# Hybrid encoder trunk: the two PSUM banks of an up chunk read as one tile, and one convolution tap on ScalarE

## The chip, the cores and the metric

The kernel runs on one core of one Trainium2 chip. The metric is device time in microseconds; lower is better. Before the change, three runs gave 2391.53, 2390.47 and 2388.43 us, median 2390.47.

## What is computed

Two layers over 256 tokens of width 2048, in float32. Each layer normalises, mixes the tokens (a bidirectional mLSTM in the first, a bidirectional gated linear recurrence, HGRN2, in the second), adds the result to the residual `h`, normalises again and goes through a gated MLP with a convolution. The change is in that MLP:

```python
def conv_glu(hn, w_up, conv_w, conv_b, w_down):
    u = hn @ w_up                                  # 2048 -> 2 x 5504
    a, v = jnp.split(u, 2, axis=-1)
    ap = jnp.pad(a, ((0, 0), (1, 1), (0, 0)))
    c = conv_b
    for j in range(3):
        c = c + ap[:, j:j + s] * conv_w[j]
    return (jax.nn.gelu(c, approximate=False) * v) @ w_down   # 5504 -> 2048
```

A final normalisation closes the trunk.

## The kernel before

**Arithmetic.** Every float32 operand of a product is split in a high and a low part in the fp32r format. ScalarE makes the high part by a cast (`parts`, L137), VectorE the low part by a subtraction (L138); products are high x high, high x low and low x high. The split activations lie in tiles of 512 columns, high parts first.

**Chunks.** The program is a list of chunks that `stream` (L282) walks through. A chunk is one output block over the whole inner dimension. In a "tm" chunk the tokens are rows of the output (L344). In a "fm" chunk the features are rows, 2 x 128 of them: for each of 16 blocks of the inner dimension and each half f, L328 multiplies the high part of the weights by both parts of the activations (512 columns: the main sum in the first 256, the low correction in the last 256), and L332 the low part of the weights by the high part (256 columns, added to the first 256). An "st" chunk is a down product by a seven-product scheme (L226 to L280), which uses all four banks of the pool `psm` and all four of `psa`.

**Weights.** Weight blocks of 2048 columns come by DMA through three `raw` buffers. They are split in pieces of 1024 columns into tiles `wh` and `wl`, four buffers of each, three pieces ahead of the matmuls (`LOOK`). A piece is four inner blocks of a fm chunk.

**PSUM.** `psm` has four tiles of one bank. A fm or tm chunk takes two of them, one per half, so that the next chunk fills the other two while the first two are read.

**Up chunks.** Each of the 86 up chunks (43 per layer, in halves of 22 and 21) gives 128 features of the gate `a` (half 0) and the same 128 of `v` (half 1). When its matmuls are recorded, `done_up`'s `go` (L1111) records the evacuation. Twice `fm_scaled` (L358): ScalarE copies the last 256 columns of the bank to SBUF (L355), VectorE adds the first 256 to it (L356) and multiplies by R, the reciprocal norm of each token (L361). Then VectorE makes the middle tap with the bias (L1118) and adds the left and right taps (L1119, L1120), ScalarE applies Gelu (L1121), VectorE multiplies by `v` (L1122), and the result is split for the down product (L1124, L1125). After some odd chunks `token_sums` (L527) makes the sums of tokens that the seven-product scheme needs.

**Beside it.** During the up chunks a side job (`prepare`, L573) loads down weights (`pth`), forms their sums on VectorE (L179 to L184) and stores them in `tscr`; the down chunks read them back. Their second splits are L209 and L210 (`th`, `tl`).

**Order.** Side jobs are stepped by `side.tick` while matmuls are recorded. What is recorded is not the order of execution: the framework's scheduler places the instructions of each engine by its own estimate of when they can run, with dependencies by tile; only instructions passed through `pin` and the loads through `late` keep the recorded order. Each engine then executes its list in order. The order of matmuls inside a fm chunk is partly set by hand with `swap` lists.

**Stages** of the profiled execution, roughly: first mixer to 380 us, up and down of layer 0 to 1092, second mixer to 1605 and its output product to 1680, up and down of layer 1 to the end. Up chunks fill 380 to 622, 746 to 986, 1680 to 1924 and 2034 to 2272.

Of the kernel before, what the change touches and what calls it, by code (L numbers as in the profile page):

```python
# [8 lines left out]
F32 = mybir.dt.float32  # L9
# [6 lines left out]
P = 128  # L16
T = 256
# [43 lines left out]
def trunk_kernel(ctx, tc, xT, x_d, fg_d, pp_d, cst_d, w_gate, w_first, w_aq, w_ak, w_av, w_ao, w_aout, w_ao2,  # L61
# [4 lines left out]
    keep = ctx.enter_context(tc.tile_pool(name="keep", bufs=1))  # L66
    wpool = ctx.enter_context(tc.tile_pool(name="wpool", bufs=1))
    ev = ctx.enter_context(tc.tile_pool(name="ev", bufs=1))
    psm = ctx.enter_context(tc.tile_pool(name="psm", bufs=4, space=PSUM))
    psa = ctx.enter_context(tc.tile_pool(name="psa", bufs=4, space=PSUM))  # L70

    pp = keep.tile([P, NPP], F32, name="pp")
# [113 lines left out]
    def split_squares(ch, parts):  # L186
# [26 lines left out]
        for u in range(units):  # L213
# [7 lines left out]
            if 2 * u + 1 < ch.nk:  # L221
                m = 512 if u in ch.seven else 1024
                wh, wl = parts(r[:, 1024:1024 + m], m)
                yield wh, wl, sums.pop(u, None)

    def squares_by_seven(ch, fetch, ready):  # L226

        psm_ = [psm.tile([P, 512], F32, tag="mm", name="mm") for _ in range(4)]
        P1, P6, P7, P5 = psm_
        C11, C12, C21, C22 = psa_ = [aux("pc") for _ in range(4)]  # L230
        begun = set()
        held.append(ch)

        def product(ps, x, w, stop):
            (xh, xl), (wh, wl) = x, w
            for i, (a, b) in enumerate(((xh, wh), (xh, wl), (xl, wh))):
                pe.matmul(ps, a, b, start=id(ps) not in begun, stop=stop and i == 2)  # L237
                begun.add(id(ps))

        def half(x, t):  # L240
            return x[:, t * P:(t + 1) * P], x[:, T + t * P:T + (t + 1) * P]

        def block(p, i):
            return tuple(w[:, i * 512:(i + 1) * 512] for w in p)

        units, last = (ch.nk + 1) // 2, max(ch.seven)
        for u in range(units):
            fetch()
            p = ready.pop(0)
            end = u == units - 1  # L250
            if 2 * u + 1 == ch.nk:
                x = ch.x(2 * u)
                for ps, t, w in ((C11, 0, 0), (C12, 0, 1), (C21, 1, 0), (C22, 1, 1)):
                    product(ps, half(x, t), block(p[:2], w), True)
                side.tick(2.7)
                break
            fetch()
            q = ready.pop(0)
            x0, x1 = ch.x(2 * u), ch.x(2 * u + 1)
            A11, A21, A12, A22 = half(x0, 0), half(x0, 1), half(x1, 0), half(x1, 1)  # L260
            B11, B22, B21 = block(p[:2], 0), block(p[:2], 1), block(q[:2], 0)
            if u in ch.seven:
                sx, t = ch.sums(u), q[2]
                S1, S3, S2, S4 = ((sx[:, i * P:(i + 1) * P], sx[:, 512 + i * P:512 + (i + 1) * P]) for i in range(4))
                T1, T3, T2, T4 = (block(t[i // 2], i % 2) for i in range(4))
                for i, (ps, x, w) in enumerate(((P1, A11, B11), (C12, S4, B22), (C11, A12, B21), (P5, S1, T1),
                                                (P7, S3, T3), (P6, S2, T2), (C21, A22, T4))):
                    product(ps, x, w, u == last and ps in psm_)
                    side.tick(0.65)
                if u == last:  # L270
                    ch.mid(psm_)
                continue
            B12 = block(q[:2], 1)
            for ps, (x, w), (y, v) in ((C11, (A11, B11), (A12, B21)), (C12, (A11, B12), (A12, B22)),
                                       (C21, (A21, B11), (A22, B21)), (C22, (A21, B12), (A22, B22))):
                product(ps, x, w, False)
                product(ps, y, v, end)
                side.tick(1.3)
        held.pop()
        ch.done(psa_)  # L280

    def stream(chunks):  # L282
        pieces = split_weights(chunks)
        ready = []

        def fetch():
            p = next(pieces, None)
            if p is not None:
                ready.append(p)

        for _ in range(LOOK):
            fetch()
        for ch in chunks:
            if ch.before:
                ch.before()
            if ch.kind == "st":
                squares_by_seven(ch, fetch, ready)
                continue
            ps = [psm.tile([P, 512], F32, tag="mm", name="mm") for _ in range(2)]
            k = 0  # L300
            while k < ch.nk:
                fetch()
                wh, wl, n = ready.pop(0)
                if ch.last and k + sum(p[2] for p in ready) + n == ch.nk:
                    pieces_, k0 = [(wh, wl, n)] + ready, k
                    for t in range(2):
                        k = k0
                        for wh, wl, n in pieces_:
                            for kk in range(n):
                                x, c = ch.x(k), slice(kk * 512, (kk + 1) * 512)  # L310
                                xh, xl = x[:, t * P:(t + 1) * P], x[:, T + t * P:T + (t + 1) * P]
                                pe.matmul(ps[t], xh, wh[:, c], start=False, stop=False)
                                pe.matmul(ps[t], xh, wl[:, c], start=False, stop=False)
                                pe.matmul(ps[t], xl, wh[:, c], start=False, stop=k == ch.nk - 1)
                                k += 1
                        ch.half(ps[t], t)
                    return
                if ch.kind == "fm":
                    ops = [(kk, f, part) for kk in range(n) for f in range(2) for part in "hl"]
                    for i in ch.swap:  # L320
                        i -= 2 * k
                        if 0 <= i < 2 * n - 1:
                            ops[2 * i + 1:2 * i + 3] = ops[2 * i + 2], ops[2 * i + 1]
                    for kk, f, part in ops:
                        x = ch.x(k + kk)
                        c = kk * ch.width + f * P
                        if part == "h":
                            pe.matmul(ps[f], wh[:, c:c + P], x, start=k + kk == 0, stop=False)  # L328
                            continue
                        if f:  # L330
                            side.tick(0.65)
                        pe.matmul(ps[f][:, 0:T], wl[:, c:c + P], x[:, 0:T], start=False, stop=k + kk == ch.nk - 1)  # L332
                    k += n
                    continue
                for kk in range(n):
                    x = ch.x(k)
                    st, sp = k == 0, k == ch.nk - 1
                    c = slice(kk * 512, (kk + 1) * 512)
                    ops = [(t, i) for t in range(2) for i in range(3)]
                    if ch.first and st:  # L340
                        ops.sort(key=lambda o: (0, 2, 1)[o[1]])
                    for t, i in ops:
                        a, w = ((0, wh), (0, wl), (T, wh))[i]
                        pe.matmul(ps[t], x[:, a + t * P:a + (t + 1) * P], w[:, c], start=st and i == 0, stop=sp and i == 2)  # L344
                    side.tick(1.3)
                    k += 1
            ch.done(ps)

    def split(dst, src, gcol, pin=lambda ins: ins):
        pin(act.activation(dst[:, 0:T], src, AF.Copy, scale=gcol))  # L350
# [746 lines left out]
    def ffn(layer, norm, nxt):  # L1097
# [12 lines left out]
        def done_up(f, i, GT, SX, seven):  # L1110
            def go(ps):  # L1111
                mp, R = box["mp"], norm.R
                avc = temporary(mp, "avc")
                a, v, c = (avc[:, j * T:(j + 1) * T] for j in range(3))
                fm_scaled(ps[0], R, a)
                fm_scaled(ps[1], R, v)
                cw = [col("conv_w", (layer * 3 + w) * FT + f) for w in range(3)]
                dve.tensor_scalar(c, a, cw[1], col("conv_b", layer * FT + f), ALU.mult, ALU.add)  # L1118
                dve.scalar_tensor_tensor(c[:, 1:T], a[:, 0:T - 1], cw[0], c[:, 1:T], ALU.mult, ALU.add)  # L1119
                dve.scalar_tensor_tensor(c[:, 0:T - 1], a[:, 1:T], cw[2], c[:, 0:T - 1], ALU.mult, ALU.add)  # L1120
                act.activation(c, c, AF.Gelu)  # L1121
                dve.tensor_tensor(c, c, v, ALU.mult)  # L1122
                g = slot(i, "g", mp)
                act.copy(g[:, 0:T], c)  # L1124
                dve.tensor_tensor(g[:, T:2 * T], c, g[:, 0:T].bitcast(F32), ALU.subtract)  # L1125
                GT.append(g)
                if i % 2 and i // 2 in seven:
                    SX[i // 2] = token_sums(mp, seven.index(i // 2), box["c"], c, avc[:, 0:2 * T])
                box["c"] = c
            return go  # L1130
# [157 lines left out]
```

## Time and profile before

| | |
|---|---|
| runs, us | 2391.53, 2390.47, 2388.43 |
| median, us | 2390.47 |
| span of the profiled execution, us | 2388.5 |
| time of that execution beyond its span | not given |
| instructions | 37988 |
| HBM read / written, MB | 512.69 / 39.91 |
| granted TensorE clock, mean | 0.999 |

The span runs from the first to the last instruction. Engines are PE (matmul), PEld (weight load, beside PE), DVE (VectorE), ACT (ScalarE), POOL (GpSimd) and SP (which issues DMAs). In a group's row stand the line, engine, operation, output<-input, sizes and count, then busy us, mean ns of one, and the idle time of the engine just before such instructions with what ended it. In a waits row stand who waited, for whom, total us, number and longest. A row of the windows view gives the stretch, its length, each engine's busy us with the number of its instructions, the granted clock, the DMA engines' share and GB/s. Matmuls overlap, and a busy TensorE is a modelled figure.

### The profile page before, as it was taken

How to read it: one execution, taken by the hardware profiler on the slowest of the kernel's cores; microseconds unless marked ns; L12 is line 12 of the kernel's file. 1: busy time of each engine (PE TensorE's matmuls, PEld its weight loads, DVE VectorE, ACT ScalarE, POOL GpSimd, SP SyncE). 2: the span in 40 equal slices, each digit the busy share in tenths (PEclk: the TensorE clock that was granted, in tenths of full speed). 3: DMA queues.
4: the chain of work that ended last, by engine and by line, in shares of the span. 5: the costliest groups of instructions: out<-in, count | busy, mean ns of one | idle time of the engine just before them, and what ended most of it. 6: DMA issues, size and time to landing. Idle time of an engine off the chain costs nothing.

```text
span 2388.5 us, 37988 instructions
## 1 busy us (share of the span) xinstructions
PE 2372.4 (99%) x14614; PEld 2030.4 (85%) x14614; DVE 1944.1 (81%) x3221; ACT 1298.8 (54%) x2013; POOL 189.7 (8%) x240
## 2 busy tenths in 40 slices
PE   9999999999999999999999999999999999999998
PEld 7888888888888888888888888888888888888887
DVE  7766687988887888777888888888889888788874
ACT  7655455454564554555555555555555565454563
POOL 0100000000000000001222222220000000000000
PEclk9999999999999999999999999999999999999999
DMA  8654556988787777755554554545798888677774
GB/s 300 201 180 165 183 178 211 333 294 317 269 293 254 251 239 262 273 194 182 173 171 168 175 177 160 177 166 188 258 325 298 298 281 296 231 249 263 249 266 148
DMA packets 98789, 555.07 MB, mean 232 GB/s; under 512 B 11168, under 2 KB 11680, under 8 KB 50736
## 3 DMA queue, kind: packets, MB, share of 16 engines
q1 hardware_dynamic: 96912, 548.64, 65.6%
q0 software_dynamic: 1120, 3.21, 0.7%
q8 instruction: 114, 1.87, 0.3%
q10 hardware_dynamic: 576, 0.79, 0.1%
q14 instruction: 67, 0.55, 0.1%
HBM read 512.69 MB, written 39.91 MB: 231 GB/s over the span
## 4 chain that ended last, share of the span: by engine, by line
PE 98%; DVE 1%; issue 1%; DMA 0%; ACT 0%; SPq 0%; POOLq 0%; POOL 0%
PE mm L328 37%; PE mm L344 23%; PE mm L332 18%; PE pc L237 12%; PE mm L237 5%; PE pn L776 1%; PE py L1034 1%; PE pd L984 1%; PE pz L405 0%; PE pa L984 0%; DMA raw<-in_w_first 0%; PE S L762 0%; DVE tl L210 0%; PE pz L1055 0%; PE pa L1009 0%
## 5 line engine op out<-in xcount | busy, mean ns | idle before, releaser
L328 PE MATMUL mm<-xt,wh 128*128 128x512 f32 x3776 | 1313.4, 394 | 0.0
L137 ACT CAST wh<-raw 128x1024 fp32r<-128x1024 f32 (+1 forms) x846 | 853.5, 1019 | 693.8 <-PE mm L328 237.9
L138 DVE TENSOR_TENSOR wl<-raw,wh 128x1024 fp32r<-128x1024 f32 (+1 forms) x846 | 1004.7, 1195 | 265.1 <-ACT wh L137 257.6
L332 PE MATMUL mm<-xt,wl 128*128 128x256 f32 x3776 | 1045.9, 278 | 0.0
L328 PEld LDWEIGHTS mm<-xt,wh 128*128 128x128 f32 x3776 | 706.2, 188 | 159.4
L332 PEld LDWEIGHTS mm<-xt,wl 128*128 128x128 f32 x3776 | 709.5, 188 | 4.5 <-issue 0.4
L344 PE MATMUL mm<-wh,xt 128*128 128x512 f32 x1024 | 320.5, 391 | 3.0 <-ACT xt L350 1.3
L344 PEld LDWEIGHTS mm<-wh,xt 128*128 128x128 f32 x1024 | 191.4, 188 | 43.3 <-ACT xt L350 1.7
L344 PE MATMUL mm<-wl,xt 128*128 128x512 f32 x512 | 198.2, 391 | 0.0
L237 PE MATMUL pc<-wh,g 128*128 128x512 f32 x508 | 167.2, 389 | 0.0
L355 ACT COPY b<-mm 128x256 f32<-128x256 f32 x236 | 87.4, 370 | 122.9 <-PE mm L332 122.7
L210 DVE TENSOR_TENSOR tl<-T,th 128x1024 fp32r<-128x1024 f32 x88 | 109.9, 1264 | 38.9 <-ACT th L209 36.7
L209 ACT CAST th<-T 128x1024 fp32r<-128x1024 f32 x88 | 92.7, 1054 | 73.6 <-PE mm L237 43.5
L237 PEld LDWEIGHTS pc<-wh,g 128*128 128x128 f32 x508 | 95.4, 188 | 19.9
L344 PEld LDWEIGHTS mm<-wl,xt 128*128 128x128 f32 x512 | 96.2, 188 | 18.9
L553 POOL TENSOR_TENSOR hm<-hm,u 128x512 f32<-128x512 f32 x8 | 10.4, 1302 | 1150.9 <-DVE u L552 1150.9
L237 PE MATMUL pc<-wl,g 128*128 128x512 f32 x254 | 98.9, 389 | 0.0
L344 PE MATMUL mm<-wh,g 128*128 128x512 f32 x308 | 96.6, 392 | 0.0
L237 PE MATMUL mm<-th,sx 128*128 128x512 f32 x264 | 91.9, 390 | 0.0
L356 DVE TENSOR_TENSOR avc<-mm,b 128x256 f32<-128x256 f32 x172 | 72.0, 418 | 14.7 <-ACT b L355 14.7
L361 DVE TENSOR_TENSOR avc<-avc,R 128x256 f32<-128x256 f32 x172 | 71.9, 419 | 1.6
L976 DVE COPY kq<-QK 128x256 f32<-128x256 f32 x224 | 69.7, 336 | 0.0
(260 smaller groups left out, 2476.7 us busy)
## 6 DMA issues: line engine op xcount, KB each, us to landing
raw<-in_w_up SPq DMA_DIRECT2D x172, 1024.0 KB, 5.5
raw<-in_w_d SPq DMA_DIRECT2D x48, 1024.0 KB, 5.0
raw<-in_w_bq SPq DMA_DIRECT2D x48, 1024.0 KB, 4.9
pth<-in_w_d SPq DMA_DIRECT2D x72, 512.0 KB, 6.7
tscr<-ptl SPq DMA_DIRECT2D x72, 512.0 KB, 4.7
T<-tscr SPq DMA_DIRECT2D x72, 512.0 KB, 5.1
raw<-in_w_d SPq DMA_DIRECT2D x36, 768.0 KB, 5.2
raw<-in_w_ao SPq DMA_DIRECT2D x24, 1024.0 KB, 4.8
```

The costliest lines, as they stand in the source:

```text
L137: pin(act.copy(wh[:, :m], r))
L138: pin(dve.tensor_tensor(wl[:, :m], r, wh[:, :m].bitcast(F32), ALU.subtract))
L209: act.copy(th, t)
L210: dve.tensor_tensor(tl, t, th.bitcast(F32), ALU.subtract)
L237: pe.matmul(ps, a, b, start=id(ps) not in begun, stop=stop and i == 2)
L328: pe.matmul(ps[f], wh[:, c:c + P], x, start=k + kk == 0, stop=False)
L332: pe.matmul(ps[f][:, 0:T], wl[:, c:c + P], x[:, 0:T], start=False, stop=k + kk == ch.nk - 1)
L344: pe.matmul(ps[t], x[:, a + t * P:a + (t + 1) * P], w[:, c], start=st and i == 0, stop=sp and i == 2)
L355: act.copy(b, ps[:, T:2 * T])
L356: dve.tensor_tensor(dst, ps[:, 0:T], b, ALU.add)
L361: dve.tensor_tensor(dst, dst, R, ALU.mult)
L976: dve.tensor_copy(m[:, j].rearrange("k (m p j) -> k m p j", p=2, j=h), blocks(z, h, 0, T))
```

## The change

A chunk's two banks become one tile of shape 128 x 2 x 512, and the pool holds two such tiles in place of four single ones. Every chunk gets its banks through the new helper `banks`; an st chunk takes both tiles. Up chunks (`paced`) hand the whole tile to `go`, other chunks the two halves. In `go`, one copy on ScalarE takes the last 256 columns of both banks into `av` (the places of `a` and `v` in the `avc` tile), one addition on VectorE adds the first 256 of both, and one multiplication scales both by R, repeated over the two halves. The middle tap with the bias moves from VectorE to ScalarE, as an Identity activation with a per-partition scale and bias.

```diff
-    psm = ctx.enter_context(tc.tile_pool(name="psm", bufs=4, space=PSUM))
+    psm = ctx.enter_context(tc.tile_pool(name="psm", bufs=2, space=PSUM))
...
+    def banks():
+        return psm.tile([P, 2, 512], F32, tag="mm", name="mm")
+
     def squares_by_seven(ch, fetch, ready):
 
-        psm_ = [psm.tile([P, 512], F32, tag="mm", name="mm") for _ in range(4)]
-        P1, P6, P7, P5 = psm_
+        P1, P6, P7, P5 = psm_ = [ps[:, i] for ps in (banks(), banks()) for i in range(2)]
...
-            ps = [psm.tile([P, 512], F32, tag="mm", name="mm") for _ in range(2)]
+            both = banks()
+            ps = [both[:, i] for i in range(2)]
...
-            ch.done(ps)
+            ch.done(both if ch.paced else ps)
...
-                fm_scaled(ps[0], R, a)
-                fm_scaled(ps[1], R, v)
+                av = avc[:, 0:2 * T].rearrange("p (a b) -> p a b", a=2)
+                act.copy(av, ps[:, :, T:2 * T])
+                dve.tensor_tensor(av, ps[:, :, 0:T], av, ALU.add)
+                dve.tensor_tensor(av, av, R.unsqueeze(1).broadcast_to([P, 2, T]), ALU.mult)
                 cw = [col("conv_w", (layer * 3 + w) * FT + f) for w in range(3)]
-                dve.tensor_scalar(c, a, cw[1], col("conv_b", layer * FT + f), ALU.mult, ALU.add)
+                act.activation(c, a, AF.Identity, bias=col("conv_b", layer * FT + f), scale=cw[1])
```

In the program as built, the counts of instructions are the same on PE, ACT, POOL and SP and 258 fewer on DVE (three for each of 86 chunks). The order differs on all engines but POOL.

## The prediction

> **What bounds the kernel now.** I read the page's engine totals and its chain first, then TensorE's waits, then the busy times cut by stage.
>
> ```profile
> PE 2372.4 (99%) x14614; PEld 2030.4 (85%) x14614; DVE 1944.1 (81%) x3221; ACT 1298.8 (54%) x2013; POOL 189.7 (8%) x240
> PE 98%; DVE 1%; issue 1%; DMA 0%; ACT 0%; SPq 0%; POOLq 0%; POOL 0%
> ```
>
> The first line is busy time by engine, the second the shares of the chain that ended last. TensorE is both. The change takes work off VectorE and puts some on ScalarE, which are neither. What can be won is therefore only time in which TensorE stands still, and the list of its waits is short:
>
> ```profile
> PE pd L984 <- issue: 2.6, 2, 1.4
> PE mm L344 <- ACT xt L350: 1.3, 1, 1.3
> PE idle L1171 <- POOL ones L1164: 1.1, 1, 1.1
> PE mm L344 <- issue: 0.9, 1, 0.9
> PE mm L344 <- ACT wh L137: 0.8, 1, 0.8
> PE mm L237 <- DVE tl L210: 0.6, 2, 0.3
> ```
>
> Columns are total us, number, longest. No wait names a line of an up chunk (L328, L332 are their matmuls). By stage, from the windows view (length, then busy us of PE, weight loads, DVE, ACT, POOL):
>
> ```profile
> 0.00:380.00 380.00, 376.75 (x2080) 317.98 (x2081) 276.37 (x481) 226.87 (x374) 20.71 (x41) 1.00 0.60 202
> 380.00:622.00 242.00, 242.00 (x1390) 211.15 (x1389) 209.89 (x354) 124.65 (x187) 0.70 (x1) 1.00 0.81 291
> 622.00:746.00 124.00, 123.69 (x564) 102.50 (x563) 102.30 (x113) 73.46 (x85) 7.09 (x4) 1.00 0.80 280
> 746.00:986.00 240.00, 240.00 (x1377) 209.55 (x1376) 199.19 (x329) 120.99 (x179) 0.00 (x0) 1.00 0.73 251
> ...
> 1092.00:1605.00 513.00, 509.50 (x4655) 439.18 (x4654) 444.55 (x913) 283.82 (x546) 138.87 (x177) 1.00 0.51 172
> 1605.00:1680.00 75.00, 74.88 (x343) 61.70 (x342) 65.41 (x91) 43.20 (x63) 4.10 (x3) 1.00 0.54 193
> 1680.00:1924.00 244.00, 244.00 (x1413) 213.44 (x1412) 214.73 (x362) 128.05 (x191) 0.70 (x1) 1.00 0.83 294
> 1924.00:2034.00 110.00, 109.74 (x486) 90.35 (x485) 89.44 (x97) 64.90 (x73) 6.54 (x4) 1.00 0.81 286
> 2034.00:2272.00 238.00, 238.00 (x1368) 207.90 (x1367) 198.81 (x325) 119.34 (x176) 2.76 (x5) 1.00 0.73 253
> 2272.00:2388.00 116.00, 107.87 (x476) 89.00 (x475) 73.40 (x87) 55.41 (x68) 4.67 (x4) 0.98 0.58 203
> ```
>
> The four stretches of up chunks are 380 to 622, 746 to 986, 1680 to 1924 and 2034 to 2272. In each TensorE's busy time equals the stretch to the last digit, although VectorE is at 83 to 88% of them. TensorE loses 3.25 us in the first mixer (380.00 - 376.75), 3.5 us in the second, 0.31 + 0.26 us in the down products behind the first up halves, 0.12 us ahead of 1680, and 8.1 us behind 2272, most of it after the last matmul. Up chunks have nothing to give back.
>
> But busy TensorE is a modelled end, so I ask whether its pace inside an up chunk bends with its neighbours' load:
>
> ```profile
> 400.00:410.00 10.00, 10.00 (x60) 8.71 (x59) 7.02 (x11) 5.30 (x7) 0.00 (x0) 1.00 0.58 201
> 410.00:440.00 30.00, 30.00 (x175) 26.25 (x174) 26.62 (x44) 15.79 (x24) 0.00 (x0) 1.00 0.89 328
> 520.00:560.00 40.00, 40.00 (x233) 34.97 (x232) 37.13 (x62) 20.33 (x32) 0.00 (x0) 1.00 0.85 304
> ```
>
> About 58 matmuls in 10 us, with one or two cut by the edges, in all three: VectorE at 70, 89 and 93%, DMA share at 0.58, 0.89 and 0.85. The pace is fixed: a pair (512 and 256 columns) every 346 ns or so (40 us over 115.5 pairs), a chunk of 32 pairs every 11.1 us.
>
> **The change part by part.** The groups that go, and the nearest rows to those that come:
>
> ```profile
> L355 ACT COPY b<-mm 128x256 f32<-128x256 f32 x236 | 87.4, 370 | 122.9 <-PE mm L332 122.7
> L356 DVE TENSOR_TENSOR avc<-mm,b 128x256 f32<-128x256 f32 x172 | 72.0, 418 | 14.7 <-ACT b L355 14.7
> L361 DVE TENSOR_TENSOR avc<-avc,R 128x256 f32<-128x256 f32 x172 | 71.9, 419 | 1.6
> L1118 DVE TENSOR_SCALAR avc<-avc,pp 128x256 f32<-128x256 f32 x86 | 34.9, 406 | 0.0
> L1020 ACT COPY AT<-pa 128x512 f32<-128x512 f32 x16 | 9.4, 587 | 0.4
> L513 DVE TENSOR_TENSOR hm<-hm,mm 128x512 f32<-128x512 f32 x14 | 9.3, 682 | 3.3 <-PE mm L344 3.3
> L534 DVE TENSOR_TENSOR sx<-avc,sx 128x512 fp32r<-128x512 f32 x26 | 17.8, 684 | 0.0
> L1121 ACT ACTIVATE avc<-avc 128x256 f32<-128x256 f32 x86 | 35.7, 415 | 42.3 <-DVE avc L1120 42.1
> L350 ACT ACTIVATE xt<-gx 128x256 fp32r<-128x256 f32 x16 | 8.1, 506 | 1.4 <-DMA gx<-in_xT 1.4
> ```
>
> *VectorE*, per chunk: out go two adds (2 x 418), two scalings (2 x 419) and the middle tap (406), 2080 ns. In come an add from PSUM over 512 elements (682, as L513) and a scaling over 512 (684, as L534): 1366 ns. It gains 714 ns, 61 us over 86 chunks; of a chunk's 11.1 us it was busy 9.6 in the first stretch (209.89/242) and is left with 8.9. All beside TensorE: 0 on the path.
>
> *ScalarE*, per chunk: two copies go (740), one of 512 columns from PSUM comes (587, as L1020). The middle tap has a per-partition scale and bias; no row has both. Gelu without either takes 415, a cast from SBUF with a scale 506, 91 more. Bounds: 415 below, 506 + 2 x 91 = 688 above; I take 506 + 91 = 597, nearest to the 506 row. So 740 goes and 1184 comes, +444 ns (262 to 535), 38 us over 86 chunks, 51 to 55% of an up stretch. Also beside TensorE: 0 on the path.
>
> *Bank pairs.* Two tiles of two banks replace four of one, so a chunk must wait until both halves of the chunk two back have been read, where a half waited for its own. Evacuation against the chunk's end:
>
> ```profile
> 468.89 0.37 ACT L355 COPY b<-mm 128x256 f32<-128x256 f32 x1 [0.71 <-PE mm L332]
> ...
> 474.16 0.42 DVE L356 TENSOR_TENSOR avc<-mm,b 128x256 f32<-128x256 f32 x1
> ```
>
> The first copy marks the chunk's last matmuls; the second half is read by 474.58, 5.7 us on, among the latest of the 86. The banks are wanted one chunk (11.1 us) later, so 5.4 us are spare, and one 682 ns add in place of two steps spends none of that. 0. If this cover went, each microsecond beyond it would stall each of 86 chunks.
>
> *The instruction order.* A scheduler places instructions, and in the program as built it places them differently on all engines but POOL. In the first chunk the matmuls no longer alternate between the two halves: the product with the low part now comes second, not third or later. That needs the low part one 512-column matmul earlier, about 0.23 us (two thirds of a pair), and it is there:
>
> ```profile
> 11.40 0.69 DVE L138 TENSOR_TENSOR wl<-raw,wh 128x512 fp32r<-128x512 f32 x1
> 12.67 0.85 PE L344 MATMUL mm<-wh,xt 128*128 128x512 f32 x3
> ```
>
> The fifth low part is done at 12.09, its block starts at 12.67. In both mixers the side products (attention, transposes) stand about ten matmuls later in TensorE's order, and VectorE's splits of weights one piece earlier against everything else. The trace of before cannot show what that costs. From below: all gaps between 380 and 2272 close, 0.31 + 3.5 + 0.12 + 0.26 = -4.2 us. From above: the mixers lose as much again as they do now, 3.25 + 3.5 = +6.8 us. I take 0, because later side products have more time for their inputs while splits ahead of evacuation delay those inputs, and both shifts are the same size. The two waits for tl sit behind a whole down product (0.3 us each), tens of microseconds after the last up chunk; a lighter up chunk does not reach them.
>
> *Sum.* The profiled span is 2388.5 us; the page does not give that execution's own time, and the median of the runs, 2390.47, lies 2.0 us above it. The sum against the span is 0, so I forecast **2390.5 us**, no change. Runs of before spread over 3.1 us.
>
> **The rivals.**
>
> *A. ScalarE's queue blocks the weight casts (slower).* The middle tap waits for VectorE's scaling, which waits for ScalarE's copy; behind it in ScalarE's order stand the casts that feed TensorE.
>
> ```profile
> L137 ACT CAST wh<-raw 128x1024 fp32r<-128x1024 f32 (+1 forms) x846 | 853.5, 1019 | 693.8 <-PE mm L328 237.9 <-PE mm L344 164.5 <-issue 151.5
> L138 DVE TENSOR_TENSOR wl<-raw,wh 128x1024 fp32r<-128x1024 f32 (+1 forms) x846 | 1004.7, 1195 | 265.1 <-ACT wh L137 257.6
> ```
>
> ```profile
> DVE ptl L179 <- DMA pth<-in_w_d: 22.7, 16, 3.9
> ```
>
> ```profile
> ACT avc L1121 <- DVE avc L1120: 42.1, 35, 3.2
> ```
>
> Casts wait mostly for a matmul to free a buffer, so they run as far ahead as four buffers allow: three pieces of eight pairs, 3 x 8 x 0.346 = 8.3 us. A cast and its split take 1.02 + 1.20, so a standstill under 6.1 us costs nothing; that is the point from which it decides. ScalarE's longest wait for VectorE in this chain is 3.2 us and VectorE's longest for a load 3.9. Both at once are 7.1, 1.0 us too long; if that met all 16 of those loads it would be 16 us: **2406**. Against it: casts stand between all steps of the new order, and today's sixteen waits cost TensorE nothing. 7%.
>
> *B. The mixers' order costs more than now (slower).* The 6.8 us above: **2397**. For it: both mixers already lose about 3 us; against: the shift gives as much as it takes. 6%.
>
> *C. Gaps close (faster).* The 4.2 us above would give **2386**; to pass 0.2% a little of the first mixer's 3.25 must go too. 4%.
>
> *D. The pace only looks fixed (faster).* If the evacuations slowed every pair, lighter VectorE work would speed it. Going from 346 to 325 ns a pair would be 21 ns x 32 x 86 = 58 us: **2333**. Against it stand the three windows, the same pace at 70 and 93% of VectorE. 2%. The Trainium skill (TensorE: Matmul & The Clock Gate, "Wait — 56ns, not 53.3ns?") puts back-to-back starts at N/2.4 + 2.5 ns, which for 512 and 256 columns is an estimate of 325 ns a pair; the trace's pairs are longer. The skill (Perfetto Trace Analysis, "Identifying the Most-Contended Engine") also calls matmul busy share a poor measure and weight-load share a good one; by that, 211 of 242 us leaves headroom that the windows do not show moving.
>
> *E. The change isn't what it says:* the merged operations last as long as two. VectorE then stays at 9.6 us a chunk and the time at 2390.5. 1%.
>
> **How the numbers follow.** No change 80% (2390.5), E 1%, A 7%, B 6%, C 4%, D 2%. Range 2386 to 2397: C's and B's ends, which are the bounds of the one unknown cost, the order; A and D lie outside with 9%. A measurement of this kernel can tell about 0.2%, 4.8 us. B's end lies above it. Faster 6%, same 81%, slower 13%.
>
> **What would show it.** Right: TensorE again busy for the whole of each up stretch; VectorE some 61 us lower in total, near 1883, ScalarE near 1337; add and scaling at about 0.68 us, the tap at about 0.6; no TensorE wait on an up chunk's line. Wrong by A: waits of L328 or L332's successors for the cast or split of weights. By B: new waits inside the mixers' windows. By D: more than 58 matmuls in 10 us of an up stretch. If the mixers' lost time changes by more than 4.8 us in either direction, my zero for the order was the failing step.

## The result

The changed kernel takes **2398.88 us** (median of 6 runs, 2396.35 to 2399.74); the kernel before took 2391.0 in the same session. The ratio is 1.0034 [1.0022, 1.0045], 8 us slower. One of the six runs of before, at 5213.07 us, lay far outside the others (2388.43 to 2391.6); the ratio is formed without such slow runs. The forecast was 2390.5 with a range of 2386 to 2397.

The profiled execution took 2399.74 us, its span is 2398.0; before, the span was 2388.5. Lines of the new kernel stand two to five further down: L331 and L335 are an up chunk's matmuls, L239 is the seven-product matmul, L549 to L557 are `mid`, L562 is `done`, L1119 to L1123 the new evacuation.

Totals and the chain by engine, from the page after:

```profile
PE 2377.9 (99%) x14614; PEld 2034.0 (85%) x14614; DVE 1904.9 (79%) x2963; ACT 1338.1 (56%) x2013; POOL 193.3 (8%) x240
PE 97%; DVE 2%; issue 1%; DMA 0%; ACT 0%; SPq 0%; POOLq 0%; POOL 0%; ACTq 0%
```

VectorE is busy 39 us less, ScalarE 39 us more, and TensorE is still the bound. The new operations, from the view of groups by line (busy us, mean ns | idle before):

```profile
L1121 DVE TENSOR_TENSOR avc<-avc,R 128x512 f32<-128x512 f32 x86 | 59.2, 688 | 1.3
L1120 DVE TENSOR_TENSOR avc<-mm,avc 128x512 f32<-128x512 f32 x86 | 58.8, 684 | 2.8 <-ACT avc L1119 2.8
...
L1123 ACT ACTIVATE avc<-avc,pp 128x256 f32<-128x256 f32 x86 | 51.6, 600 | 46.1 <-DVE avc L1121 45.4
...
L1119 ACT COPY avc<-mm 128x512 f32<-128x512 f32 x86 | 49.8, 579 | 3.4 <-DVE g L1130 3.4
```

Forecast were 684, 682, 597 and 587 ns. The up chunks did what the change says. Now TensorE's waits in the new kernel:

```profile
PE mm L239 <- ACT wh L137: 2.4, 2, 1.7
PE pc L239 <- DVE hm L562: 2.2, 2, 1.2
PE mm L347 <- ACT xt L353: 1.7, 1, 1.7
PE mm L239 <- DVE u L551: 1.5, 1, 1.5
PE mm L239 <- DVE tl L210: 1.1, 1, 1.1
```

These are the five longest rows of ten. Four of them stand at L239, the matmuls of the seven-product scheme; the one at L347 is at the start of the program. No row names an up chunk for an operation of the evacuation. The windows view, cut at the same times as before, says the same (stretch, length, then busy us of PE, weight loads, DVE, ACT, POOL, the clock, DMA):

```profile
0.00:380.00 380.00, 376.71 (x2069) 317.92 (x2070) 273.81 (x478) 226.21 (x371) 21.64 (x41) 1.00 0.60 200
380.00:622.00 242.00, 242.00 (x1389) 211.41 (x1388) 201.11 (x292) 133.81 (x187) 0.70 (x1) 1.00 0.82 294
622.00:746.00 124.00, 121.32 (x548) 100.48 (x548) 95.71 (x106) 72.97 (x86) 2.54 (x2) 0.99 0.78 276
746.00:986.00 240.00, 240.00 (x1376) 209.41 (x1375) 193.27 (x265) 129.03 (x175) 4.02 (x2) 1.00 0.71 245
...
1092.00:1605.00 513.00, 512.84 (x4664) 442.19 (x4663) 444.37 (x911) 283.45 (x537) 140.09 (x176) 1.00 0.52 175
1605.00:1680.00 75.00, 72.92 (x334) 58.73 (x333) 63.26 (x92) 43.58 (x70) 4.26 (x3) 1.00 0.51 173
1680.00:1924.00 244.00, 244.00 (x1405) 213.43 (x1404) 204.45 (x295) 135.46 (x188) 0.70 (x1) 1.00 0.82 295
1924.00:2034.00 110.00, 107.30 (x483) 88.70 (x482) 86.50 (x93) 67.41 (x77) 2.55 (x2) 1.00 0.80 288
2034.00:2272.00 238.00, 238.00 (x1360) 207.50 (x1359) 189.39 (x260) 125.72 (x171) 6.60 (x6) 1.00 0.71 244
```

The up stretches are full, with VectorE lower by 6 to 10 us in each. TensorE now stands for 2.68 us in 622 to 746 (0.31 before), 2.08 in 1605 to 1680 (0.12) and 2.70 in 1924 to 2034 (0.26): all three hold down or output products with the seven-product scheme. The second mixer went the other way, from 3.50 us to 0.16.

All kernels here issue the same number of matmuls in the chunks, so the start of the k-th can be set against the k-th of before. The table gives that lag in us for each profiled execution, at points named by before's own time. It is where the rest of this section and the experiments are read from.

| kernel | 32 | 399 | 625 | 713 | 1134 | 1617 | 1663 | 1913 | 2001 | last |
|---|---|---|---|---|---|---|---|---|---|---|
| after | 2.0 | 2.1 | 2.1 | 6.2 | 6.5 | 2.9 | 6.2 | 6.1 | 8.6 | 9.7 |
| e1 tap only | -0.4 | -0.4 | -0.4 | -0.3 | -0.3 | 0.2 | 0.2 | 0.2 | 0.2 | 0.2 |
| e2 pair tiles only | 0.1 | 0.6 | 0.6 | 4.7 | 5.0 | 1.7 | 5.0 | 4.9 | 9.1 | 10.2 |
| e3 pairs in up chunks | -0.9 | 0.0 | 4.1 | 4.3 | 4.4 | 0.4 | 0.4 | 5.4 | 5.7 | 5.7 |
| e4 pairs in st chunks | -0.5 | 5.2 | 5.4 | 7.9 | 7.9 | 9.0 | 16.9 | 15.6 | 18.1 | 18.1 |
| e5 other partner | 0.0 | 0.5 | 0.5 | 5.1 | 5.4 | 2.0 | 4.2 | 4.2 | 6.8 | 7.9 |
| e6 e3 + exchange | -1.0 | -0.2 | 0.1 | 0.1 | 0.1 | -4.2 | -4.1 | -2.9 | -2.9 | -2.8 |
| e7 e3 - exchange | 2.1 | 3.2 | 7.3 | 7.5 | 7.5 | 3.4 | 3.4 | 8.4 | 8.6 | 8.6 |
| e8 before - exchange | -0.3 | -0.2 | 4.0 | 5.0 | 5.0 | 4.4 | 4.4 | 8.6 | 8.8 | 8.8 |
| e9 before, copy of P6 | -0.6 | -0.7 | -0.7 | 3.1 | 3.1 | 5.9 | 6.3 | 5.8 | 6.1 | 6.1 |
| e10 copy on VectorE | 0.0 | 0.5 | 0.5 | 5.2 | 5.6 | 2.1 | 5.4 | 5.3 | 10.0 | 11.1 |
| e11 e6, old evacuation | -0.8 | 0.2 | 0.5 | 0.5 | 0.5 | -3.3 | -3.3 | -1.7 | -1.4 | -1.4 |

The changed kernel loses 4.1 us between 625 and 713, 3.3 between 1617 and 1663, 2.5 between 1913 and 2001 and 1.1 behind 2001, and wins 3.6 between 1134 and 1617, the second mixer. So some 11 us are lost and under 4 won. The win goes with pair tiles in the up chunks: all eight kernels that have them gain 3.3 to 4.3 us there, and e1, e4, e8 and e9, which have not, gain at most 0.6. The 2.0 at the start is no part of the change: e2 has the same tiles and 0.1, e7 has 2.1 where its near twin e3 has -0.9.

**The place itself.** Layer 0's passage from its first down product to its second, ScalarE in the kernel before (start, us, operation):

```profile
679.42 0.59 ACT L546 COPY u<-mm 128x512 f32<-128x512 f32 x1
...
688.48 1.06 ACT L209 CAST th<-T 128x1024 fp32r<-128x1024 f32 x1 [4.57 <-PE mm L237]
690.07 1.57 ACT L137 CAST wh<-raw 128x1024 fp32r<-128x1024 f32 x2 [0.53 <-PE pc L237]
```

VectorE there: P1's addition, one of `done` (L559), and the first of P5's:

```profile
681.80 0.68 DVE L547 TENSOR_TENSOR hm<-hm,mm 128x512 f32<-128x512 f32 x1
...
686.95 0.68 DVE L559 TENSOR_TENSOR hm<-hm,pc 128x512 f32<-128x512 f32 x1
688.03 0.69 DVE L549 TENSOR_TENSOR hm<-hm,mm 128x512 f32<-128x512 f32 x1 [0.41 <-PE mm L237]
```

And ScalarE in the kernel after:

```profile
690.57 1.06 ACT L209 CAST th<-T 128x1024 fp32r<-128x1024 f32 x1 [4.26 <-PE mm L239]
691.53 0.58 ACT L549 COPY u<-mm 128x512 f32<-128x512 f32 x1
692.45 1.05 ACT L209 CAST th<-T 128x1024 fp32r<-128x1024 f32 x1 [0.35 <-DMA T<-tscr]
693.41 1.56 ACT L137 CAST wh<-raw 128x1024 fp32r<-128x1024 f32 x2
```

`u` copies P1, whose last matmul comes early in the product. Before, it was copied at 679.42. Now P1 lies in one tile with P6, the last of the single-use products, and is copied 12 us later, behind P6. The weight casts that open the next product start at 693.41 in place of 690.07. Of both delays 2.1 us are the lag that this execution already had, so the copy is 10 us later within the passage and the casts 1.2. The casts also stand behind one `th` more, the split of a stored weight sum (692.45); before, that split came behind them (692.38). VectorE after shows the bunch: P5's two additions, P1's, and the one of `u`, with splits between them.

```profile
690.57 0.69 DVE L552 TENSOR_TENSOR hm<-hm,mm 128x512 f32<-128x512 f32 x1 [1.83 <-PE mm L239]
691.18 0.68 DVE L554 TENSOR_TENSOR hm<-hm,mm 128x512 f32<-128x512 f32 x1
691.78 1.22 DVE L210 TENSOR_TENSOR tl<-T,th 128x1024 fp32r<-128x1024 f32 x1
692.91 0.68 DVE L550 TENSOR_TENSOR hm<-hm,mm 128x512 f32<-128x512 f32 x1
693.51 0.68 DVE L551 TENSOR_TENSOR u<-u,mm 128x512 f32<-128x512 f32 x1
694.11 1.22 DVE L210 TENSOR_TENSOR tl<-T,th 128x1024 fp32r<-128x1024 f32 x1
695.24 0.68 DVE L562 TENSOR_TENSOR hm<-hm,pc 128x512 f32<-128x512 f32 x1
```

And TensorE stands, first for the cast, then for a `pc` bank that L562 at 695.24 sets free. The third row is the same passage in layer 1:

```profile
694.50 0.50 PE L239 MATMUL mm<-wh,g 128*128 128x512 f32 x1 [1.70 <-ACT wh L137]
695.98 0.51 PE L239 MATMUL pc<-wh,g 128*128 128x512 f32 x1 [0.98 <-DVE hm L562]
...
1987.92 0.47 PE L239 MATMUL mm<-wh,g 128*128 128x512 f32 x1 [1.53 <-DVE u L551]
```

The cast ended at 694.45, but the bank was hardly earlier. In layer 1 the same matmul waits for L551, the addition that reads P6 out of the tile which the next P1 needs; here L551 ended at 694.19. Before, P1 had a tile of its own, which L547 had read by 682.48. The first addition of `done`, which frees a `pc` bank, is late too: 695.24 in place of 686.95.

The two stands are 2.68 us. The rest of the 4.1 is TensorE's clock (the number behind POOL's), after and then before:

```profile
694.00:698.00 4.00, 2.52 (x8) 1.87 (x9) 4.00 (x6) 0.97 (x2) 0.00 (x0) 0.91 0.86 310
698.00:702.00 4.00, 4.00 (x13) 3.12 (x13) 2.54 (x5) 0.89 (x1) 2.54 (x2) 0.66 0.63 205
...
697.40:700.60 3.20, 3.20 (x9) 2.50 (x8) 2.31 (x5) 0.00 (x0) 1.57 (x2) 0.50 0.57 164
```

```profile
694.00:698.00 4.00, 4.00 (x19) 3.15 (x18) 4.00 (x3) 2.15 (x3) 3.54 (x2) 1.00 0.71 227
698.00:702.00 4.00, 3.69 (x17) 2.66 (x16) 4.00 (x6) 2.10 (x3) 0.00 (x0) 1.00 0.70 235
```

While it was low the clock stood at a half, as the third row shows. So 0.91 and 0.66 of 4 us each mean 0.7 + 2.7 = 3.4 us at a half, 1.7 us lost. 2.68 + 1.7 less the 0.3 that before lost there as well is 4.1. In layer 1 the stands, 1.53 and 1.17 us, are as long and the clock stays at 1.00, so the loss there is 2.5. The third place, 1617 to 1663, has stands of 0.70 us (for a cast), 1.14 (for `tl`) and 0.16 (for L551), 2.0 of its 3.3 us; the rest was not traced.

### The profile page after: what moved, and what is told of

It is laid out like the page before. It is cut to its first block, busy times and chain, and to the rows that moved or that the text cites. A ratio compares the mean times of both kernels' runs of the same rounds, so it can differ in the third digit from the quotient of the medians.

```text
span 2398.0 us, 37828 instructions
## 1 busy us (share of the span) xinstructions
PE 2377.9 (99%) x14614; PEld 2034.0 (85%) x14614; DVE 1904.9 (79%) x2963; ACT 1338.1 (56%) x2013; POOL 193.3 (8%) x240
## 4 chain that ended last, share of the span: by engine, by line
PE 97%; DVE 2%; issue 1%; DMA 0%; ACT 0%; SPq 0%; POOLq 0%; POOL 0%; ACTq 0%
PE mm L331 36%; PE mm L347 23%; PE mm L335 18%; PE pc L239 11%; PE mm L239 5%; PE pn L779 1%; PE py L1037 1%; DVE wl L138 1%; PE pd L987 0%; PE pz L408 0%; PE pa L987 0%; DVE tl L210 0%; DMA raw<-in_w_first 0%; PE S L765 0%; PE pz L1058 0%
## 5 line engine op out<-in xcount | busy, mean ns | idle before, releaser
L331 PE MATMUL mm<-xt,wh 128*128 128x512 f32 x3776 | 1313.9, 394 | 0.2 <-issue 0.2
L335 PE MATMUL mm<-xt,wl 128*128 128x256 f32 x3776 | 1048.2, 279 | 0.0
L331 PEld LDWEIGHTS mm<-xt,wh 128*128 128x128 f32 x3776 | 707.0, 188 | 160.6 <-issue 0.5
L335 PEld LDWEIGHTS mm<-xt,wl 128*128 128x128 f32 x3776 | 710.4, 188 | 4.1 <-issue 0.4
L347 PE MATMUL mm<-wh,xt 128*128 128x512 f32 x1024 | 323.9, 393 | 2.2 <-ACT xt L353 1.7
L347 PEld LDWEIGHTS mm<-wh,xt 128*128 128x128 f32 x1024 | 192.3, 189 | 42.2 <-ACT xt L353 2.1
L347 PE MATMUL mm<-wl,xt 128*128 128x512 f32 x512 | 200.9, 393 | 0.0
L239 PE MATMUL pc<-wh,g 128*128 128x512 f32 x508 | 168.3, 391 | 2.2 <-DVE hm L562 2.2
L210 DVE TENSOR_TENSOR tl<-T,th 128x1024 fp32r<-128x1024 f32 x88 | 105.1, 1220 | 43.1 <-ACT th L209 42.4
L239 PEld LDWEIGHTS pc<-wh,g 128*128 128x128 f32 x508 | 95.7, 188 | 22.6 <-DVE hm L562 2.8
L347 PEld LDWEIGHTS mm<-wl,xt 128*128 128x128 f32 x512 | 96.6, 189 | 19.0
L239 PE MATMUL pc<-wl,g 128*128 128x512 f32 x254 | 99.1, 390 | 0.0
L347 PE MATMUL mm<-wh,g 128*128 128x512 f32 x308 | 96.3, 391 | 0.0
L239 PE MATMUL mm<-th,sx 128*128 128x512 f32 x264 | 92.5, 391 | 0.0
L1123 ACT ACTIVATE avc<-avc,pp 128x256 f32<-128x256 f32 x86 | 51.6, 600 | 46.1 <-DVE avc L1121 45.4
L1005 POOL TENSOR_TENSOR G<-G 128x384 f32<-128x384 f32 (+2 forms) x96 | 67.8, 706 | 6.3
L347 PEld LDWEIGHTS mm<-wh,g 128*128 128x128 f32 x308 | 57.8, 188 | 12.0
```

The source lines that it names most:

```text
L210: dve.tensor_tensor(tl, t, th.bitcast(F32), ALU.subtract)
L1005: pool.tensor_tensor(G2, G[:, 0:6 * n:2], G[:, 1:6 * n:2], ALU.mult)
L1123: act.activation(c, a, AF.Identity, bias=col("conv_b", layer * FT + f), scale=cw[1])
```

## The experiments

Two theories stood at first. **T:** the pair tiles make the readings of a down product wait for the later of two banks; they bunch at its end and hold up the next product. The rivals to it: the middle tap on ScalarE, or the merged evacuation. A second question came up with e3, and with it theory **R** and its rival S. Each kernel was timed in five rounds with the kernel before beside it; before's medians in the three sessions of experiments were 2390.76 (e1 to e4), 2389.99 (e5 to e8) and 2389.91 (e9 to e11).

**e1: the tap alone.** The kernel before with one line changed:

```diff
-                dve.tensor_scalar(c, a, cw[1], col("conv_b", layer * FT + f), ALU.mult, ALU.add)
+                act.activation(c, a, AF.Identity, bias=col("conv_b", layer * FT + f), scale=cw[1])
```

> The kernel before with the middle tap on ScalarE and nothing else. Theory T (the loss comes from the bank pairs in the down product: P1 shares a tile with P6, so its early reading waits for P6's last matmul, and the eight operations behind it fall together at the end of the down product): as before, 2390 to 2392 us, no gap of TensorE over 0.5 us at the two passages from one down product to the next (about 690 and 1985 us). Rival A (ScalarE's queue is held up by the tap): most of the 8 us, 2396 to 2399. Rival S (start-up chance: a load that lands late lets the TensorE clock fall for one 3.4 us stretch, 1.7 to 2.2 us): 2390 or 2392 by chance, in this kernel as in any other.

Measured 2391.4 us, ratio 1.0004 [0.9995, 1.0013]. The tap costs nothing that these runs can tell, and its lag shows none of the losses.

**e2: the tiles alone.** Pair tiles everywhere, evacuation and tap as before:

```diff
-                fm_scaled(ps[0], R, a)
-                fm_scaled(ps[1], R, v)
+                fm_scaled(ps[:, 0], R, a)
+                fm_scaled(ps[:, 1], R, v)
```

> The changed kernel's bank pairs everywhere, but the evacuation of an up chunk half by half as before and the middle tap on VectorE. Theory T: the full loss, 2396 to 2400 us, with the reading of P1 some 12 us later than before in all eight down products and TensorE gaps of 1 to 2 us at about 692 and 1987 us. Rival A or any theory that puts the loss in the merged operations: 2390 to 2392.

Measured 2399.94 us, ratio 1.0036 [1.0023, 1.0048]: the whole loss, without one merged operation. The copy of P1 is later in all eight products, by some 3 to 10 us beyond the lag and not by the 12 expected. The waits are those of the changed kernel:

```profile
PE mm L239 <- ACT wh L137: 2.7, 2, 2.0
PE pc L239 <- DVE hm L562: 1.8, 2, 1.2
PE mm L239 <- DVE u L551: 1.5, 1, 1.5
```

**e3: pair tiles in up chunks alone.** The whole change there; all other chunks take single tiles from a pool that is opened and closed at the border:

```diff
+    def layout_for(paired):
+        if psm["paired"] != paired:
+            psm["stack"].close()
+            psm["pool"] = psm["stack"].enter_context(tc.tile_pool(name="psp" if paired else "pss", bufs=2 if paired else 4, space=PSUM))
+            psm["paired"] = paired
...
+            layout_for(ch.paced)
```

> All of the change in the up chunks (pair tiles, merged copy, addition, scaling, tap on ScalarE), but every other chunk, the down products included, has four tiles of one bank; the pool is closed and opened again where the two kinds meet. Theory T: the loss is gone, 2389 to 2393 us, P1 read early again. Rival (the merged operations or the new order in the up chunks): 2396 to 2400. If the passage from up chunk to down product now costs a wait for the whole pool: up to 1 us at each of four passages, seen in the waits.

Measured 2396.78 us, ratio 1.0026 [1.0016, 1.0036]. The losses at the three places of the down products are gone (lags 4.1 to 4.3, 0.4 to 0.4, 5.4 to 5.7), as T has it, but 4.1 us came between 399 and 625 and 5.0 between 1663 and 1913, where the changed kernel loses nothing. That was expected by no theory. The windows show it: TensorE is full and issues fewer matmuls. The first row is in layer 0's first up half, the second in its second:

```profile
520.00:560.00 40.00, 40.00 (x229) 34.68 (x228) 32.84 (x46) 20.47 (x28) 0.00 (x0) 1.00 0.78 276
860.00:900.00 40.00, 40.00 (x232) 34.99 (x232) 33.25 (x49) 22.64 (x32) 0.00 (x0) 1.00 0.71 241
```

229 against the 233 of before. From the starts, a pair of a 512- and a 256-column matmul takes 346.7 ns in before and in the second half here, and 353.3 ns in the first half: 6.6 ns x 16 blocks x 2 halves x 22 chunks = 4.6 us for a half throughout. The expected cost of the change of pool shows as four short waits, 1.0 us in all, two at the start of each layer's first up chunk.

**e4: pair tiles in st chunks alone**, with the same switching of pools (`layout_for(ch.kind == "st")`) and single tiles in up chunks.

> The kernel before with pair tiles in the down products alone, single tiles and the old evacuation everywhere else. Theory T: the loss without any other part of the change, 2395 to 2400 us, gaps at about 692 and 1987 us as in the changed kernel. Rival: 2390 to 2392, as before.

Measured 2411.87 us, ratio 1.0087 [1.0073, 1.0101], above the 2395 to 2400 of T. It is slower without any part of the change in an up chunk; but more than T gives, since here the pool changes at the edges of each down product and a chunk with single tiles waits for all of `mid`:

```profile
PE mm L356 <- DVE u L564: 5.8, 2, 2.9
PE mm L248 <- DVE u L560: 3.1, 2, 1.5
PE pc L248 <- DVE hm L571: 2.3, 2, 1.2
```

(L356 is the matmul of a tm chunk in this kernel.) The steps that stay inside a run of st chunks, 625 to 713 and 1913 to 2001, are 2.5 each. So the sign is T's, the size is partly the experiment's own.

**e5: other partners.** The changed kernel with P1 beside P5, the second to end, in place of P6:

```diff
-        P1, P6, P7, P5 = psm_ = [ps[:, i] for ps in (banks(), banks()) for i in range(2)]
+        P1, P5, P7, P6 = psm_ = [ps[:, i] for ps in (banks(), banks()) for i in range(2)]
...
-            P1, P6, P7, P5 = ps
+            P1, P5, P7, P6 = ps
```

> The changed kernel, with the four single-use products of a seven-product chunk paired otherwise: P1 with P5 and P7 with P6, where the change pairs P1 with P6 and P7 with P5. P5 is the second of them to end, P6 the last, so P1's early reading waits for less. Theory T (a pair tile is read only when both its banks are written, so the readings of a down product bunch at its end): part of the loss goes, as one more reading moves ahead of the last products; between 2392 and 2398 us, I take 2395, and the step of about 4 us between 692 and 712 us shrinks. Rival (pair tiles cost the same however they are paired, because of the number of banks that are free): 2399 us as the changed kernel.

Measured 2395.51 us, ratio 1.002 [1.0011, 1.003]: where T expected it, though the interval still meets the changed kernel's, [1.0022, 1.0045], so that the rival isn't excluded by the time. And the step of 625 to 713 did not shrink (4.6 us); what shrank in the profiled execution, the slowest of its runs at 2397.91, is 1617 to 1663, from 3.3 to 2.2. That half of the expectation failed. ScalarE and TensorE at the passage show why:

```profile
692.59 1.04 ACT L209 CAST th<-T 128x1024 fp32r<-128x1024 f32 x1 [2.73 <-DMA T<-tscr]
...
694.64 0.78 PE L239 MATMUL mm<-wh,g 128*128 128x512 f32 x1 [3.40 <-ACT wh L137]
```

The copy of P1 is early, at 688.33. But the split of a stored sum still stands ahead of the weight casts, as in the changed kernel, and here it waits for its load. So the order of ScalarE's list, and not only the late readings, holds up the next product.

**Theory R, e6 to e8.** R: the stream of matmuls has two steady rhythms, and the order of a few matmuls where it starts sets which one holds. S: the two-bank operations slow each pair. The list `swap` exchanges neighbouring matmuls. In the cut below the comment names the runs. e6 is e3 with one exchange more, e7 is e3 with one fewer, e8 is the kernel *before* with one fewer and nothing else:

```diff
-  swap=(2,) if part and i == 0 else (3,) if f0 + i == 1 else (), paced=True))
+  swap=(2,) if part and i == 0 else (3,) if f0 + i in (1, 3) else (), paced=True))      # e6
+  swap=(2,) if part and i == 0 else (), paced=True))                                    # e7, e8
```

> The kernel with pair tiles and the whole change in up chunks alone, and one more exchange of two neighbouring matmuls in the fourth chunk of each layer's first up half. Theory R (the stream of matmuls has two steady rhythms, 346.7 and 353.3 ns a pair, and the order of a few matmuls at its start sets which one holds): the rhythm can flip; if it does, the first halves lose about 4 us each and the time is near 2388.5 us, else 2396.8. Rival S (the merged operations on two banks slow each pair, whatever the order): 353.3 ns again, 2396.8 us.

> The same kernel without the exchange in the second chunk of the first up halves. Theory R: either rhythm, 2388.5 or 2396.8 us, and at least one of this run and of that with one exchange more differs from 353.3 ns a pair. Rival S: 353.3 ns and 2396.8 us.

> The kernel before, without the exchange in the second chunk of the first up halves; nothing else. Theory R: the order alone can bring the slow rhythm, then 353.3 ns a pair in both first up halves (or one) and about 2398.5 us (4 us a half); where the exchange does not matter, 346.7 ns and 2390.8. Rival S: the kernel before has no merged operations, so 346.7 ns and 2390.8 us.

Measured: e6 2388.14 us, ratio 0.9994 [0.9985, 1.0002]; e7 2396.31, 1.0028 [1.0016, 1.0039]; e8 2398.53, 1.0036 [1.0023, 1.0049]. The same 40 us in e6 and then in e8:

```profile
520.00:560.00 40.00, 40.00 (x233) 34.99 (x232) 32.86 (x45) 21.53 (x31) 0.00 (x0) 1.00 0.79 276
```

```profile
520.00:560.00 40.00, 40.00 (x228) 34.70 (x227) 33.99 (x55) 19.49 (x29) 0.00 (x0) 1.00 0.78 274
```

R holds, S falls: the kernel before, with its own evacuation, drops to the slow rhythm when one exchange of neighbours goes, and the merged evacuation gets the fast one when one is added. In the traces of before and e8, the instructions of TensorE, VectorE, ScalarE and GpSimd come in the same order but for these two pairs of matmuls. In e6, whose new exchange is in the fourth chunk, the second and third chunk still take 352.8 and 353.1 ns a pair, and every chunk behind the fourth 346.7. So one exchange sets the pace of the chunks behind it; the 20 chunks of e8 make 4.2 us in each of two halves.

**e9: only the copy late, with single tiles.** The kernel before, where ScalarE's copy takes P6 and VectorE then adds P1:

```diff
-            act.copy(u, P1)
+            act.copy(u, P6)
...
-            dve.tensor_tensor(u, u, P6, ALU.add)
+            dve.tensor_tensor(u, u, P1, ALU.add)
```

> The kernel before with its single tiles; in a seven-product chunk's mid operations ScalarE's first copy reads P6, the last product to end, in place of P1, the first, and VectorE then adds P1 in place of P6. The sum is the same. Theory T, sharpened (ScalarE's copy u stands in its queue until P6 ends, and the weight cast that the next product needs first stands behind it): the loss of the changed kernel's down products appears without any pair tile, up to 4 us at 692 to 712 us and up to 2.5 us near 1987, 2393 to 2398 us. Rival (pair tiles cost something as such, with fewer tiles to hand out): no pair tile, so 2390.5 us.

Measured 2392.06 us, ratio 1.0011 [1.0002, 1.0019]: 2.1 us without any pair tile, above the rival's 2390.5 and below T's 2393 to 2398, so neither forecast was met. The profiled execution was the slowest of its runs (2396.4) and can't be taken as typical; in it the passage lost 3.8 us, yet not in T's way. TensorE stood there for `th`, the split of a stored weight sum that itself came late by DMA, as ScalarE's row shows:

```profile
694.03 1.04 ACT L209 CAST th<-T 128x1024 fp32r<-128x1024 f32 x1 [3.09 <-DMA T<-tscr]
```

The copy stands at 688.73 there, and the weight casts behind it start at 689.37, no later than before (690.07). So the 2.1 us are shown for the edit, but not a way in which the late copy makes them.

**e10: the copy on VectorE.** The changed kernel with `dve.tensor_copy(u, P1)` in place of `act.copy(u, P1)`.

> The changed kernel with the copy u of a seven-product chunk on VectorE in place of ScalarE. Theory T, sharpened: the weight casts no longer queue behind it, but VectorE's splits do, and VectorE is as bunched as before; the passage's loss shrinks from 4.1 us but needn't go, 2394 to 2398 us. Theory T in its first form (all the readings bunch at the end, the engine of one of them matters little): 4 us there still, 2399 us.

Measured 2400.34 us, ratio 1.0047 [1.0034, 1.0059]. The sharper form of T, that the weight casts queue behind this copy, falls: without it on ScalarE the passages of both layers lose 4.7 us. The first form fits: all readings are late, and whichever engine carries the copy, the next product waits. The `th` split is ahead of the weight casts here too (690.77 and 691.73), and at layer 1's passage TensorE waits for L551.

**e11: what the merged operations are worth.** e6 with the old evacuation and the tap on VectorE; pair tiles and exchanges stay.

> Pair tiles in up chunks alone, with the exchange in the second and fourth chunk of the first up halves, as in the run that gave 2388.1 us, but with the old evacuation: four copies and adds and two scalings of 256 columns, middle tap on VectorE. It shows what the merged operations and the tap are worth by themselves. If VectorE's and ScalarE's load beside TensorE is free, as the prediction had it: the same 2388 us within 2, unless the rhythm of the matmul stream flips, which adds about 4 us for each first half. Rival (the lighter VectorE is what won the 2 us against the kernel before): 2390 us or more, with TensorE waits that the other run doesn't have.

Measured 2389.01 us, ratio 0.9999 [0.999, 1.0008]. e6 has 0.9994 [0.9985, 1.0002]. 61 us of instruction time off VectorE make 0.9 us between the medians, less than the intervals of some 2 us to either side can tell from nothing. What both kernels win against before comes in the second mixer (lags of -4.2 and -3.3 at 1617), with and without the merged operations.

e6 is the best version that the experiments point to. It beats the changed kernel by some 10 us (0.9994 against 1.0034). Against the kernel before it is not distinguished: its interval reaches over 1.

## Why the prediction was wrong

**What bounds the kernel: right.** TensorE is full in the up stretches, and nothing that these runs can tell came back of what was taken off VectorE there (e11 against e6).

**VectorE and ScalarE: right in each duration and in "0 on the path"** (e1 for the tap, e11 for the evacuation). VectorE's total was misjudged: 61 us were to go, 39 went. The rows say why. In the VectorE timeline above an addition of 0.69 us is followed 0.61 us after its start: neighbours overlap by some 0.08 us. Durations count that twice, busy time once; 258 instructions fewer x 0.08 = 21 us, which is about the difference of 22. ScalarE's 1338.1 answers to the 1337 forecast.

**"Bank pairs ... 0": this step failed, and it is the loss.** It asked when the banks of an up chunk are *free* for the chunk after next, and found 5.4 us to spare; that holds. It did not ask what else a tile of two banks joins: the moment at which either half may be *read*. In an up chunk both halves end together, and no loss shows there. The st chunk was in the diff, with four banks that end at different times and the earliest beside the latest in one tile. Nor did it put its own question to that chunk, which takes both tiles: the next product's P1 must wait until P6 is read, and TensorE waits for just that reading, L551, 1.53 us in layer 1. In the trace of before the early reading stood in plain sight at 679.42, 8.6 us ahead of P5's additions at 688.03. e2 shows that the tiles alone bring the loss, e3 and e6 that it goes when st chunks keep single tiles. In the terms of the sum: the pairs were put at 0, and cost some 11 us in the products of the seven-product scheme, against which the second mixer gave back under 4.

**"The instruction order ... 0": not the step that made the loss, and wrong as a separate term.** By its own sign it stands: the mixers' lost time moved by 3.3 us, less than the 4.8 it named. Its lower end, that the second mixer's 3.5 us of gaps close, came true almost to the full (3.50 to 0.16 us of standing). Its upper end put losses into the mixers; the losses are in the down products and come from the tiles. The prediction took the scheduler's new order as a thing by itself, with a gain and a loss of one size. It is what the dependency makes of it: in the built program, `u`'s copy stands behind two weight casts more in ScalarE's list (248 in place of 246 for this product) and behind three `th` splits more (21 in place of 18).

**"The pace is fixed": right of neighbours' load, wrong as a rule.** Windows at 70 to 93% of VectorE's time showed one pace, and e11 against e6, with the same 233 matmuls in 40 us at 34.75 and 32.86 us of VectorE, confirms that this load does not matter. But there are two paces, 346.7 and 353.3 ns, and the order of matmuls chooses. The changed kernel stayed in the fast one, so this cost the forecast nothing; in e3 and e8 it is worth 8 us, as much as the whole change.

**The rivals.** None named the mechanism. A had the right shape, a cast behind an instruction that waits, but in the up chunks, where the margin holds. B (2397) had the wrong place: the first mixer lost as much as before, the second less; that 2398.88 lies near its time is chance. C's gap closed, and was outweighed. D and E fell.

**What stays open.** How the loss divides between the bank that L551 frees late, the weight casts behind one `th` more, and the additions of `done` is not settled: in the changed kernel the first two end within 0.3 us of each other, and no run takes one away alone. The rival of e5, that fewer tiles to hand out cost as such, is not excluded by its time. Why pair tiles in the up chunks close the second mixer's gaps was not traced. Why one order leads to one rhythm and not to the other was not found; the runs only show that it does.

## What to carry to other kernels

When two buffers become one, ask of every user, not only of the one that the change is for, two things: when is the later half free, and when may the earlier half be read; the second is found by listing the first readings of each buffer against the last writes of its new partner. Work taken off an engine that the bound engine does not wait for was worth nothing measurable here, while the same edit moved the order of everything else: budget that first. Where a fully busy engine issues a few per mille fewer instructions in equal windows, compare start-to-start intervals before blaming the neighbours.

## What the hardware showed

A stand of 1.70 + 0.98 us cost about 1.7 us more, because the granted clock then fell for some 3.4 us; the same happened at the start of the profiled execution, where 8 to 12 and 12 to 16 us have 0.90 and 0.67 and before has 1.00. The Trainium skill (TensorE: Matmul & The Clock Gate, "Part 1: The HAM clock gate") gives half rate after at least one idle window of about 3.4 us and full rate after a busy one. The length agrees; but TensorE was busy for 2.52 of the 4 us in which the fall lies, and its longest stand ahead of it was 1.70 us, so a wholly idle window was not needed here. Nor did such stands always do it: the 1.53 and 1.17 us of layer 1 left the clock at 1.00.

```profile
1990.00:1994.00 4.00, 4.00 (x20) 3.29 (x19) 3.09 (x6) 0.94 (x1) 1.38 (x2) 1.00 0.63 184
```

The clock records of all thirteen traces change only at whole multiples of 3.413 us from the first change of the run. Counted by these steps, the clock never fell behind one in which TensorE stood for 1.59 us or less, always (8 of 8) behind one with 1.79 us or more, and in 4 of 6 cases in between (1.63 to 1.72). So in these runs a fall went with the sum of the stands within one step, from about half of it on.

A stream of alternating 512- and 256-column matmuls, all with weight loads, ran at 346.7 or at 353.3 ns a pair with nothing waiting, each steady for some 200 us, and one exchange of two neighbours, in the second or the fourth chunk, chose between them.
